# First feed forward's output product in Strassen's form, the norm after it fed by halves of the tokens, and two smaller rearrangements

## The chip, the cores and the metric

One NeuronCore of a Trainium2 chip runs the whole program. The metric is the device time of one execution in microseconds. In the profile PE is the matrix engine (TensorE), PEld its weight loads, DVE is VectorE, ACT is ScalarE, POOL is GpSimd, and SP is the engine whose queue starts nearly all transfers.

## The reference

One layer of a hybrid decoder, on 1024 prompt tokens and 32 sample tokens (8 sequences of 4), which the kernel treats as one block of T = 1056 columns. D is 1024, the feed forward's hidden width DFF is 2816, everything is float32.

```
x = x + 0.5 * SwiGLU_1(RMSNorm(x))
h = RMSNorm(x);  z = h @ w_in          # conv pair | q | k | v | gates
x = x + w_out( sigmoid(g_A) * conv(z) + sigmoid(g_B) * attention(z) )
x = x + 0.5 * SwiGLU_2(RMSNorm(x))
SwiGLU(h) = (silu(h @ w_gate) * (h @ w_up)) @ w_ffn_out
```

Outputs are x, the new keys and values, and the updated caches, most of them copies.

## The kernel before, in words

Features lie on the 128 partitions and tokens in the free dimension; x is eight tiles (KT = 8) of 128 x 1056. To keep float32 precision, each product of two float32 tiles is done as three TensorE products: both operands are split into a rounded high part (ACT, `activation` Copy into F32R) and a low remainder (a subtraction on DVE or POOL), and hi*hi, hi*lo and lo*hi are summed in PSUM. `weights` (L157), `split` (L183), `gemm` (L173) do this; the split of the weights is most of POOL's work.

The stages in order are these.

- **Start of the first feed forward**, `load_x` (L206). x comes in nine row blocks, is transposed on TensorE, and 1/rms of each token is a column that `scale(tb)` spreads over the partitions: ACT makes a diagonal matrix `dg` (L262), TensorE multiplies it by ones (L267), DVE copies the PSUM result to the SBUF row `rb` (L268). `apply` (L367) then makes h = x * gain * rb by one DVE instruction for each tile and block of 352 tokens (L373), its high part on ACT (L375) and its low part (L378). The hidden columns j = 0 and 1 are computed in the plain form, block by block (`lockstep` L444, `plain_gate`, `plain_up`, `plain_out` L468). `plain_last` (L476) does the last of these, splits its weights on DVE and issues `first_sums` (L542), the first weight sums of the next stage. The engines keep the program's order here (`in_order`, L117); what is issued after it, such as `combine` (L494), may be put between by the scheduler.
- **Hidden stage**, `hidden` (L430): for j = 2 to 21, `hidden_fast` (L553) does gate and up together by Strassen's form: 8 products of four K-tiles on two halves of 264 columns, 168 matmuls for each j. The sums of weights s1 to s4 (L564 to L567) and the four results `C` lie in one tile `q` of the tag "quad" (5 buffers), taken anew for each j.
- **Output product.** The first feed forward does it plainly, `ffn_out` (L804): 22 K-tiles in 4 chunks, 8 output tiles, 3 blocks of 352 columns, three products: 1584 matmuls. In the last chunk `after` calls `norm_feed` for each output tile and block: `scaled` (L354: a Copy on ACT, a remainder on DVE L359) and `square` (L382: ACT, and an addition on POOL L390 into the row `rbn`). The second feed forward does it by Strassen's form, `ffn_out_fast` (L661): K-tiles in pairs, in three passes of 4, 4 and 3 pairs, 7 products each, 4 output pairs o, two halves b of 264 columns, three products: 1848 matmuls. For that its hidden stage also forms differences of hidden rows on POOL (`hidden_pair` L624, L630 to L637) and stores them to `hx`. `acc` (L761) adds a product to x on DVE, `more` (L764) adds a kept term on POOL.
- **Mixer**: `norm_end` (L412) sums `rbn` over partitions, `qkv` (L1061), attention, convolution, gates, `branches`.
- **`mix_out`** (L1511): the mixer's output product, then 1/rms by `rms` (L392: a matmul with ones, a square root on ACT, a reciprocal on DVE L398, all on 128 x 352) and the start of the second feed forward in the same shape as `load_x`'s, in the order written out by hand.
- Hidden stage and `ffn_out_fast` of the second feed forward, the latter ending in `store_y` (transposes, L855).

Background work is issued by `later(n, ...)` n products ahead, `tick` counts products.

## Time and profile before

| | us |
|---|---|
| median of 3 runs | 2376.51 |
| lowest, highest | 2375.69, 2379.31 |
| the profiled execution | 2374.05 |
| its span | 2372.3 |

The span runs from the first to the last instruction of the profile; the execution's own time is 1.75 us more. A row of stretches gives, for each engine, its busy time and its instructions (x), then the granted TensorE clock as a share of full speed, the DMA engines' busy share and their rate. A row of waits says who waited for whom, the sum in us, how often, and the longest. A row of groups gives line, engine, operation, output<-inputs, shape, count, then busy us and mean ns of one, then idle us before them and what ended it. A row of the timeline gives start and length in us, and in brackets the idle time before it and what ended that.

### The profile page before, as it was taken

The page shows a single profiled execution, that of the slowest core. Times are in us where ns is not written, and L with a number is a line of the kernel's source. Part 1 is how long each engine was busy: PE and PEld are TensorE (multiplying, and loading weights), DVE is VectorE, ACT ScalarE, POOL GpSimd, SP SyncE. Part 2 cuts the span into 40 slices and gives each one's busy share as a digit, 9 for nine tenths or more (in the row PEclk, how much of TensorE's full clock was granted, in tenths as well). Part 3 has the DMA queues.
Part 4 walks back from the last instruction along what each step waited for, and adds up shares of the span by engine and source line. Part 5 has one row for each costly group of instructions (what it writes and reads, how often), then busy time and mean ns, then how long its engine had stood idle before and what let it go on. Part 6 is the DMA issues. An engine that isn't in the chain of part 4 may idle for free. (4 is left out here: it accounts for less than half of the span.)

```text
span 2372.3 us, 43139 instructions
## 1 busy us (share of the span) xinstructions
PE 2291.5 (97%) x16725; PEld 2231.9 (94%) x16725; DVE 1304.1 (55%) x2420; ACT 871.1 (37%) x2193; POOL 1143.6 (48%) x1070
## 2 busy tenths in 40 slices
PE   7999999999999999999999999998999999999998
PEld 7899999999999998987998999998999999999998
DVE  6755555542234635686666846418644434467765
ACT  5322222341125643643644234224332223234443
POOL 5644444453325512422421354545755555567676
PEclk8999999999999999999999999999999999999999
DMA  6222222273434212222243434631334333366323
GB/s 206 85 78 73 82 82 82 71 249 126 145 94 141 53 43 67 78 73 91 76 120 97 145 103 129 215 98 61 103 104 136 121 125 116 110 250 207 106 88 102
DMA packets 279705, 268.50 MB, mean 113 GB/s; under 512 B 21101, under 2 KB 254277, under 8 KB 277668
## 3 DMA queue, kind: packets, MB, share of 16 engines
q1 hardware_dynamic: 269292, 245.42, 32.5%
q10 hardware_dynamic: 10208, 20.32, 2.6%
q8 instruction: 132, 2.16, 0.4%
q14 instruction: 73, 0.60, 0.1%
HBM read 197.58 MB, written 87.27 MB: 120 GB/s over the span
## 5 line engine op out<-in xcount | busy, mean ns | idle before, releaser
L178 PE MATMUL mm<-h,wh 128*128 128x352 f32 x2256 | 566.2, 332 | 2.7 <-DVE t L1481 1.8
L578 PE MATMUL acc<-h,wh 128*128 128x264 f32 x2560 | 478.7, 287 | 23.5 <-DVE quad L587 14.8
L578 PEld LDWEIGHTS acc<-h,wh 128*128 128x128 f32 x2560 | 400.9, 190 | 28.1 <-issue 17.7
L178 PEld LDWEIGHTS mm<-h,wh 128*128 128x128 f32 x2256 | 401.6, 192 | 9.2 <-issue 2.6
L178 PE MATMUL mm<-h,wl 128*128 128x352 f32 x1128 | 371.9, 330 | 2.3 <-DVE wl L168 2.3
L578 PE MATMUL acc<-h,wl 128*128 128x264 f32 x1280 | 366.4, 286 | 0.0
L185 POOL TENSOR_TENSOR wl<-quad,wh 128x512 fp32r<-128x512 f32 x156 | 208.3, 1340 | 304.7 <-ACT wh L184 280.4
L578 PE MATMUL acc<-quad,wh 128*128 128x264 f32 x1920 | 354.5, 285 | 0.0
L168 POOL TENSOR_TENSOR wl<-wr,wh 128x512 fp32r<-128x512 f32 (+2 forms) x156 | 193.0, 1252 | 326.5 <-ACT wh L167 312.4
L578 PEld LDWEIGHTS acc<-quad,wh 128*128 128x128 f32 x1920 | 297.6, 188 | 0.2
L578 PE MATMUL acc<-quad,wl 128*128 128x264 f32 x960 | 272.7, 284 | 0.0
L578 PEld LDWEIGHTS acc<-h,wl 128*128 128x128 f32 x1280 | 243.2, 190 | 0.0
L754 PE MATMUL mm<-quad,wh 128*128 128x264 f32 x1232 | 230.3, 288 | 8.6 <-POOL quad L185 3.1
L1087 PE MATMUL mm<-wh,h 128*128 128x256 f32 x1152 | 219.8, 286 | 0.0
L178 PEld LDWEIGHTS mm<-h,wl 128*128 128x128 f32 x1128 | 217.0, 192 | 2.6 <-DVE wl L168 2.6
L184 ACT ACTIVATE wh<-quad 128x512 fp32r<-128x512 f32 x156 | 96.2, 628 | 304.9 <-DVE quad L565 165.6
L185 POOL TENSOR_TENSOR wl<-wr,wh 128x512 fp32r<-128x512 f32 x124 | 170.3, 1375 | 75.7 <-ACT wh L184 75.6
L754 PEld LDWEIGHTS mm<-quad,wh 128*128 128x128 f32 x1232 | 191.9, 189 | 11.1 <-issue 4.5
L1087 PEld LDWEIGHTS mm<-wh,h 128*128 128x128 f32 x1152 | 181.2, 189 | 1.2 <-issue 0.6
L578 PEld LDWEIGHTS acc<-quad,wl 128*128 128x128 f32 x960 | 180.6, 188 | 0.0
L754 PE MATMUL mm<-quad,wl 128*128 128x264 f32 x616 | 175.9, 286 | 1.4 <-POOL wl L185 1.4
L167 ACT ACTIVATE wh<-wr 128x512 fp32r<-128x512 f32 x196 | 107.7, 574 | 165.8 <-PE mm L178 101.1
(289 smaller groups left out, 4226.8 us busy)
## 6 DMA issues: line engine op xcount, KB each, us to landing
wr<-ffn_w_in SPq DMA_DIRECT2D x88, 512.0 KB
wr<-w_in SPq DMA_DIRECT2D x42, 512.0 KB
quad<-hx SPq DMA_DIRECT2D x74, 264.0 KB
xd<-quad SPq DMA_DIRECT2D x24, 528.0 KB
t<-hd SPq DMA_DIRECT2D x66, 176.0 KB
hd<-quad SPq DMA_DIRECT2D x20, 528.0 KB
hx<-quad SPq DMA_DIRECT2D x10, 1056.0 KB
quad<-xd SPq DMA_DIRECT2D x16, 528.0 KB
```

Source lines behind the costliest of these rows:

```text
L167: nc.scalar.activation(hi, raw[:, k:k + m, :], AF.Copy)
L168: ins = (eng or nc.gpsimd).tensor_tensor(out=lo, in0=raw[:, k:k + m, :], in1=f(hi), op=ALU.subtract)
L178: self.nc.tensor.matmul(ps[:, :BW], p, x[:, blk(tb)], start=(k == 0 and i == 0), stop=(k == nk - 1 and i == 2))
L184: self.nc.scalar.activation(hi, src, AF.Copy)
L185: return (eng or self.nc.vector).tensor_tensor(out=lo, in0=src, in1=f(hi), op=ALU.subtract)
L578: nc.tensor.matmul(acc[:, b, :HB], p[:, k, :], x[:, cols], start=(first and k == 0 and i == 0), stop=(k == 3 and i == 2), skip_group_check ...
L754: nc.tensor.matmul(ps[:, :HB], wp[:, k, :], q[:, s, k, cols], start=(k == 0 and i == 0), stop=(k == n - 1 and i == 2))
L1087: nc.tensor.matmul(ps[:m, :256], x, w, start=(k == 0 and j == 0), stop=(k == 7 and j == 2))
```

## The change

`build` calls `ffn_out_fast` for the first feed forward too, with its own last pass order, with `hx` rows in DRAM of its own, and with hooks that feed the mixer's norm by halves of the tokens. 1/rms is read by `apply` from PSUM. The tiles of `C` are taken twice and kept. `first_sums` is issued earlier, and every part of `combine` has to follow the split of u1.

```diff
+ORDER_END1 = ("P1", "P6", "P7", "P5", "P4", "P3", "P2")
@@ load_x
-        rb = self.rb = self.new_rb()
-            return lambda: nc.vector.tensor_copy(rb[:, 384 * tb:min(384 * tb + 384, T)], pb[:, :min(384, T - 384 * tb)])
+            return self.spread([(max(BW * tb - 128 * i, 0), min(BW * tb + BW - 128 * i, size(i)), rs[:, i:i + 1])
+                                for i in range(9) if 128 * i < BW * tb + BW and 128 * i + size(i) > BW * tb])
...
-            elif k == 7:
-                out.append(scale(2))
-        self.apply(gname, 1, second)
-        out.pop()()
+        self.apply(gname, 1, rb1, second)
         lock1 = self.lockstep(g0, u0, 1)
         for k in range(KT):
+            if k == 5:
+                rb2 = scale(2)
             lock1(k)
@@ apply
-                                               in1=self.rb[:, blk(tb)], op0=ALU.mult, op1=ALU.mult)
+                                               in1=rb[:, :BW], op0=ALU.mult, op1=ALU.mult)
+    def spread(self, parts):
+        pb = self.sc_ps()
+        n = 0
+        for a, b, col in parts:
+            dg = self.small(128, "dg", 3)
+            nc.scalar.activation(dg[:b, :b], self.ident[:b, :b], AF.Copy, scale=col[:b])
+            nc.tensor.matmul(pb[:, n:n + b - a], self.ones[:b, :], dg[:b, a:b], start=True, stop=True)
+            n += b - a
+        return pb
+    def square_half(self, k, h):
+        for t in (2 * HB * h, 2 * HB * h + HB):
+            x, s = self.xT[k][:, t:t + HB], self.rbn[:, t:t + HB]
+            if t not in self.squared:
+                self.squared.add(t)
+                nc.scalar.activation(s, x, AF.Square)
+            else:
+                sq = self.t352()[:, :HB]
+                nc.scalar.activation(sq, x, AF.Square)
+                nc.gpsimd.tensor_tensor(out=s, in0=s, in1=sq, op=ALU.add)
+    def scaled_half(self, gname, k, h):
+        sl = slice(2 * HB * h, 2 * HB * h + 2 * HB)
...
+        nc.scalar.activation(hi, x, AF.Copy, scale=g)
+        nc.vector.scalar_tensor_tensor(out=lo, in0=x, scalar=g, in1=f(hi), op0=ALU.mult, op1=ALU.subtract)
@@ plain_last
         self.u1_end = self.split_end
+        self.first_sums(w_in)
...
-            if tb == 1:
-                self.first_sums(w_in)
@@ combine
-            if k == 0:
-                self.after(ins, self.u1_end)
+            self.after(ins, self.u1_end)
@@ hidden_fast
-        q = self.quad().rearrange("p a t -> p (a t)")
+        if j < NREG + 2:
+            self.cs.append(self.quad().rearrange("p a t -> p (a t)"))
+        q = self.cs[j % 2]
...
+        if j == NREG:
+            self.after(ins, self.plain_end)
@@ ffn_out_fast
+            if last and p == end[0] and begin is not None:
+                begin()
+            ws = None
+            if middle is not None and step == len(order) - 1:
+                ws = [parts(o) for o in range(4)]
+                middle()
+            for o in range(4):
+                hi, lo = ws[o] if ws else parts(o)
...
                     if p == "P1":
-                        u[o, b] = self.t352()[:, :HB] if c else u12
-                        nc.scalar.activation(u[o, b], ps[:, :HB], AF.Copy, scale=0.25)
+                        u[o, b] = self.t352()[:, :HB] if c and not last else u12
+                        if last:
+                            acc(u12)
+                        else:
+                            nc.scalar.activation(u[o, b], ps[:, :HB], AF.Copy, scale=0.25)
...
                     elif p == "P6":
                         acc(u[o, b])
-                        if c:
+                        if c and not last:
                             more(u12, u[o, b])
                         if last:
                             more(x22, u12)
                     elif p == "P7":
+                        if last and end is not ORDER_END:
+                            more(x21, u12)
@@ qkv
-            for i in range(9):
+            for i in ((5, 6, 7, 8, 0, 1, 2, 3, 4) if g == 0 and kind == "q" else range(9)):
@@ mix_out
+        def rms(tb):
+            ps, r = self.tr_ps(), self.small(3, "r3", 2)
+            for i in range(3):
...
+                nc.tensor.matmul(ps[:m, i:i + 1], self.rbn[:, c:c + m], self.ones[:, 0:1], start=True, stop=True)
+                parts.append((0, m, r[:, i:i + 1]))
+            for m, c in ((128, slice(0, 2)), (BW - 256, slice(2, 3))):
+                nc.scalar.activation(r[:m, c], ps[:m, c], AF.Sqrt, scale=1.0 / D, bias=self.eps[:m])
+                nc.vector.reciprocal(r[:m, c], r[:m, c])
+            return lambda: self.spread(parts)
-        self.rms(0)()
-        left = [part(o, tb) for o, tb in ((6, 1), (7, 1), (5, 2))]
+        rb0 = rms(0)
+        left = [part(6, 1)]
+        rb0 = rb0()
+        left += [part(o, tb) for o, tb in ((7, 1), (5, 2))]
...
         p = self.plain_gate(w[2], 0)
+        rb.append(todo.pop(0)())
@@ build
+            self.hx = self.pairs("hy")
             self.hidden(a["ffn1_w_in"][0])
+            def final(o, h):
+                nc.sync.dma_start(out=self.xd[1][o][:, h * 2 * HB:h * 2 * HB + 2 * HB], in_=self.xT[o][:, h * 2 * HB:h * 2 * HB + 2 * HB])
+                self.square_half(o, h)
+                if o >= 4 or h == 0:
+                    self.scaled_half("mix_norm", o, h)
+            def middle():
+                for o in range(4):
+                    self.scaled_half("mix_norm", o, 1)
-            self.ffn_out(a["ffn1_w_out"][0], after, self.norm_begin)
+            self.ffn_out_fast(a["ffn1_w_out"][0], final, ORDER_END1, self.norm_begin, middle)
```

## Rows read from the trace of the kernel before

**Rows 1.** Stretches: starts, hidden stages, output products; PE, PEld, DVE, ACT, POOL.

```profile
0.00:88.98 88.98, 68.40 (x378) 65.58 (x379) 67.06 (x90) 45.47 (x91) 52.80 (x56) 0.88 0.48 154
88.98:505.50 416.52, 413.30 (x3360) 412.51 (x3360) 216.13 (x264) 127.25 (x217) 192.08 (x150) 0.99 0.29 91
505.50:761.90 256.40, 255.51 (x1585) 255.54 (x1585) 84.93 (x153) 73.58 (x162) 97.39 (x103) 1.00 0.44 142
...
1604.00:1683.98 79.98, 69.44 (x413) 67.89 (x411) 70.20 (x77) 35.91 (x68) 55.28 (x41) 0.97 0.17 56
1683.98:2114.50 430.52, 416.84 (x3360) 412.92 (x3360) 192.76 (x263) 130.94 (x228) 249.71 (x188) 0.99 0.38 127
2114.50:2206.17 91.67, 84.73 (x673) 83.63 (x673) 73.31 (x105) 37.32 (x67) 66.84 (x41) 0.98 0.68 230
2206.17:2290.04 83.87, 82.52 (x672) 81.95 (x673) 58.36 (x101) 34.29 (x62) 57.11 (x43) 1.00 0.29 94
2290.04:2372.30 82.26, 74.20 (x592) 71.11 (x592) 47.28 (x106) 30.45 (x62) 56.28 (x59) 1.00 0.35 103
```

**Rows 2.** Stretches without a stall inside the plain and the Strassen output product.

```profile
561.00:700.00 139.00, 139.00 (x865) 139.00 (x864) 37.04 (x70) 25.92 (x61) 42.42 (x46) 1.00 0.39 125
2242.68:2277.79 35.11, 35.11 (x288) 35.11 (x289) 21.46 (x42) 13.41 (x23) 27.41 (x23) 1.00 0.26 86
```

**Rows 3.** Groups on POOL by form, third pass of the Strassen output product.

```profile
L764 POOL TENSOR_TENSOR quad<-quad,wr 128x264 f32<-128x264 f32 x24 | 19.3, 814 | 0.5
L185 POOL TENSOR_TENSOR wl<-h,wh 128x384 fp32r<-128x384 f32 x17 | 17.7, 1047 | 5.0 <-ACT wh L184 5.0
L185 POOL TENSOR_TENSOR quad<-quad 128x528 fp32r<-128x528 f32 x10 | 13.6, 1368 | 0.0
```

**Rows 4.** Groups on DVE by form, last chunk of the plain output product.

```profile
L359 DVE SCALAR_TENSOR_TENSOR h<-quad,mix_norm,h 128x352 fp32r<-128x352 f32 x23 | 13.7, 598 | 14.0 <-ACT h L358 13.9
L838 DVE SCALAR_TENSOR_TENSOR quad<-mm,quad 128x352 f32<-128x352 f32 x25 | 13.1, 524 | 16.9 <-PE mm L178 16.9
```

**Rows 5.** Stretches: fourth and fifth product of the second feed forward's third pass.

```profile
2316.90:2330.21 13.31, 11.55 (x89) 10.46 (x88) 9.54 (x24) 5.40 (x10) 13.15 (x16) 1.00 0.30 89
2330.21:2344.14 13.93, 12.00 (x95) 10.87 (x93) 6.40 (x16) 5.20 (x11) 13.93 (x16) 1.00 0.42 123
```

**Rows 6.** Waits of PE and of DVE, second feed forward's hidden stage.

```profile
PE acc L578 <- DVE quad L587: 11.7, 10, 1.9
...
DVE quad L564 <- DMA hx<-quad: 36.8, 17, 4.1
```

**Rows 7.** Timeline of DVE and of PE, one such wait.

```profile
1890.56 0.69 DVE L564 TENSOR_TENSOR quad<-wr 128x512 f32<-128x512 f32 x1 [2.09 <-DMA hx<-quad]
...
1892.01 0.48 PE L578 MATMUL acc<-h,wh 128*128 128x264 f32 x2 [1.85 <-DVE quad L587]
```

**Rows 8.** Timeline of PE, first start: the longest idle time.

```profile
42.41 1.79 PE L267 MATMUL sc<-dg,ones 128*128 128x128 f32 x6 [6.41 <-ACT dg L262]
```

**Rows 9.** Stretches after the long idle times: first start, second start.

```profile
42.40:50.00 7.60, 7.58 (x32) 7.30 (x33) 6.03 (x10) 2.45 (x6) 2.58 (x3) 0.65 1.02 406
1655.00:1684.00 29.00, 24.64 (x142) 24.38 (x142) 26.13 (x30) 12.74 (x23) 22.52 (x14) 0.92 0.10 35
```

**Rows 10.** Waits of PE, end of the first start.

```profile
PE acc L578 <- DVE t L469: 2.4, 1, 2.4
```

**Rows 11.** Waits of PE, `mix_out` and second start.

```profile
PE mm L453 <- DVE t L460: 4.5, 1, 4.5
PE acc L578 <- DVE t L469: 4.2, 1, 4.2
```

**Rows 12.** Groups on DVE by form, second start, then first start.

```profile
L373 DVE SCALAR_TENSOR_TENSOR quad<-quad,ffn_norm,rb 128x352 f32<-128x352 f32 x24 | 21.8, 945 | 0.1
L398 DVE RECIPROCAL rb<-rb 128x352 f32<-128x352 f32 x3 | 7.0, 2348 | 2.6 <-ACT rb L397 2.5
...
L511 DVE TENSOR_TENSOR quad<-quad,quad 128x528 f32<-128x528 f32 x4 | 5.4, 1362 | 0.0
```

More of the change, by code (lines that the diff above doesn't have):

```diff
@@ L256, in scale @@
         def scale(tb):
-            d = []
-            for i in range(3 * tb, 3 * tb + 3):
-                m = size(i)
-                dg = self.small(128, "dg", 3)
-                nc.scalar.activation(dg[:m, :m], self.ident[:m, :m], AF.Copy, scale=rs[:m, i:i + 1])
-                d.append((i, m, dg))
-            pb = self.sc_ps()
-            for i, m, dg in d:
-                c = (i - 3 * tb) * 128
-                nc.tensor.matmul(pb[:, c:c + m], self.ones[:m, :], dg[:m, :m], start=True, stop=True)
-            return lambda: nc.vector.tensor_copy(rb[:, 384 * tb:min(384 * tb + 384, T)], pb[:, :min(384, T - 384 * tb)])
+            return self.spread([(max(BW * tb - 128 * i, 0), min(BW * tb + BW - 128 * i, size(i)), rs[:, i:i + 1])
+                                for i in range(9) if 128 * i < BW * tb + BW and 128 * i + size(i) > BW * tb])
         n0 = self.here()
@@ L275, in load_x @@
             turn(i)()
-        scale(0)()
+        rb0 = scale(0)
         g0, u0 = (self.weights(w_in[:, c:c + 128], KT, 128, sent=in_turn) for c in (0, DFF))
@@ L290, in first @@
                 out.append(turn(2 + k // 2))
-        self.apply(gname, 0, first, FIRST_K)
+        self.apply(gname, 0, rb0, first, FIRST_K)
         lock(KT - 1)
@@ L324, in third @@
                 keep.append(self.plain_swish(q))
-        self.apply(gname, 2, third)
+        self.apply(gname, 2, rb2, third)
         lock2 = self.lockstep(g0, u0, 2)
@@ L410, in norm_feed @@
         self.square(k, tb)
+    def square_half(self, k, h):
+        nc = self.nc
+        for t in (2 * HB * h, 2 * HB * h + HB):
[8 more added lines that the diff above has]
+    def scaled_half(self, gname, k, h):
+        nc = self.nc
+        if self.hn[k] is None:
+            self.hn[k] = (self.hrow(), self.hrow())
+        sl = slice(2 * HB * h, 2 * HB * h + 2 * HB)
+        x, g = self.xT[k][:, sl], self.gain[gname][:, k:k + 1]
+        hi, lo = (r[:, sl] for r in self.hn[k])
+        nc.scalar.activation(hi, x, AF.Copy, scale=g)
+        nc.vector.scalar_tensor_tensor(out=lo, in0=x, scalar=g, in1=f(hi), op0=ALU.mult, op1=ALU.subtract)
     def norm_end(self, cols):
@@ L438, in hidden @@
         self.two_banks()
+        self.cs = []
         for j in range(NREG, DFF // 128):
@@ L659, in pair_src, with ffn_out_fast @@
         return self.hx[i][t][:, r, :]
-    def ffn_out_fast(self, w_out, final):
+    def ffn_out_fast(self, w_out, final, end=ORDER_END, begin=None, middle=None):
         nc = self.nc
@@ L701, in ffn_out_fast @@
         X = {}
-        order = [(c, p) for c in range(len(PAIRS)) for p in (ORDER if c < len(PAIRS) - 1 else ORDER_END)]
+        order = [(c, p) for c in range(len(PAIRS)) for p in (ORDER if c < len(PAIRS) - 1 else end)]
         loads = []
@@ L742, in ffn_out_fast, with parts @@
                 load_x(*order[step + 2])
-            for o in range(4):
+            last = c == len(PAIRS) - 1
+            if last and p == end[0] and begin is not None:
+                begin()
+            def parts(o):
                 hi = self.P.tile([128, 4, 128], F32R, name=self.nm("wh"), tag="wh", bufs=6)
@@ L772, in ffn_out_fast @@
                         acc(x12)
-                        if last:
+                        if last and end is ORDER_END:
                             more(x21, u12)
@@ L1561, in first @@
             elif k == 7:
-                todo.pop(0)()
+                rb.append(todo.pop(0)())
                 w.append(weight(0))
                 left.append(part(7, 2))
-        self.apply(g, 0, first)
+        rb = []
+        self.apply(g, 0, rb0, first)
         left.pop(0)()
@@ L1577, in second @@
             elif k == 4:
-                todo.append(self.rms(2))
+                todo.append(rms(2))
             elif k == 5:
                 self.plain_up(lock0, 0, 0)
-            elif k == 8:
-                todo.pop(0)()
-        self.apply(g, 1, second)
+        self.apply(g, 1, rb[0], second)
         p = self.plain_gate(w[2], 0)
+        rb.append(todo.pop(0)())
         lock1 = self.lockstep(*w[:2], 1)
@@ L1593, in third @@
                 self.plain_up(lock1, 1, 0)
-        self.apply(g, 2, third)
+        self.apply(g, 2, rb[1], third)
         keep.append(self.plain_swish(self.plain_gate(w[2], 1)))
@@ L1641, in mixer, with pairs @@
         self.gates(0, 16, PR['gdrain'])
+    def pairs(self, name):
+        return [[self.DR.tile([128, n, 2 * HB], F32, name=f"{name}{i}_{n}") for n in (2, 4, 1)] for i in range(DFF // 256)]
     def build(self):
@@ L1675, in build @@
             self.mix_out(mg)
-            self.hx = [[self.DR.tile([128, n, 2 * HB], F32, name=f"hx{i}_{n}") for n in (2, 4, 1)] for i in range(DFF // 256)]
+            self.hx = self.pairs("hx")
             self.copy_caches(1, *COPY2)
```

18 lines of the change are left out of this document (9 added, 9 removed).

## The prediction

> **What bounds the kernel now.** I read the stretches first, cut at the borders of the stages, then the waits inside the stretches in which PE is not full, then the prices. PE is the bound almost everywhere: in the first hidden stage it is busy 413.30 of 416.52 us, in the plain output product 255.51 of 256.40. What it loses lies in few places: 20.6 us in the first start, 10.5 in the second, 13.7 in the second hidden stage, and 16.3 in the Strassen output product with its end [rows 1]. So a change pays either by fewer PE columns or by closing these holes, and this one does some of both.
>
> **The output product.** The plain form streams 1584 matmuls of 352 columns; an undisturbed stretch has 139.00 us for 864 of them, 160.9 ns each, so 254.8 us, about what the stage takes. The Strassen form needs 1848 of 264 columns; undisturbed, 288 take 35.11 us, 121.9 ns each [rows 2], so 225.3 us. PE alone would give back 30 us. The same code in the second feed forward shows how much of that survives. Its first pass takes 91.67 us where 672 x 121.9 ns are 81.9, its second 83.87 [rows 1]. I take both as they stand, since the first feed forward issues the same weight, x and operand transfers in the same order; the bounds are 10 us less in the first pass (its transfers arrive in time) and nothing more.
>
> The third pass is where the two feed forwards differ. PE needs 504 x 121.9 ns = 61.4 us. In the second feed forward it takes 82.26 us with 88 transposes and the end, and POOL is busy 56.28 us in it [rows 1]; its fourth and fifth products, 13.31 and 13.93 us instead of 8.8 and the transposes, have POOL busy all but 0.16 us [rows 5]. In the first, transposes fall away, but the norm comes in: 16 squares of half rows make 32 activations on ACT and 28 additions on POOL (the first of each quarter of the tokens needs none), and 16 `scaled_half` of 528 columns. An addition on 264 columns costs POOL 0.81 us by the nearest row, L764 [rows 3], so 22.8 us; the eight additions that P1's `acc` on DVE makes needless save 6.5. POOL then has 56.28 - 6.5 + 22.8 = 72.6 us of work against PE's 61.4. Its queue is in order and also makes the low parts of weights (1.05 us) and operands (1.37 us) [rows 3], which PE waits for. The last product's eight additions (6.5) can lie behind PE's end; 66 cannot. I take 70 us: 61.4 (nothing late) and 82 (see the rivals) are the bounds. Sum of the stage: 91.7 + 83.9 + 70 = 245.5 against 256.4, **-11 us**, between -31 and 0. That is a third of what PE alone promises.
>
> DVE has 47.28 us in the second feed forward's third pass [rows 1]; eight more `acc` and 16 remainders of 528 columns at 598 ns x 528/352 = 0.90 us [rows 4] add 3.2 and 14.4, so 65 us: nearly full too. Here a rule speaks against the change. The remainder of 352 columns with both tensors in SBUF takes 598 ns while POOL works half the time, one with an operand in PSUM 524 [rows 4], and `apply`'s with both in SBUF 945 where POOL is busier [rows 12]. The Trainium skill's page SBUF — State Buffer, section Who interferes with whom, says that a DVE instruction with two SBUF inputs and a GpSimd instruction that reads SBUF use one read interface, and that the later one waits for the whole of the other. By that rule DVE's 16 remainders would each wait out a POOL instruction; rival A prices this from the rows.
>
> The handover to the mixer: after the last product the chain is `acc`, square, addition for two halves, some 0.4 + 0.4 + 2 x 0.8 = 2.4 us, and the sums over partitions are issued behind one product of the mixer, 24 x 0.12 = 2.9 us. With POOL behind I book **+1.5**, between 0 and 6. The new order of q's tiles (5 to 8 first) only takes tokens that are ready; the x stores become 16 halves on SP's queue and the loads of q's weights lie among them: nothing, unless SP holds those loads behind the last stores, which is within the 6.
>
> **The first hidden stage** now forms the differences for Strassen: in the second feed forward these make POOL's time 249.71 instead of 192.08 us, and SP's traffic 127 instead of 91 GB/s [rows 1], both far from full. On PE they cost nothing by themselves: **+1**, between 0 and +14, the difference of the two hidden stages.
>
> **C's tiles kept.** The second hidden stage takes 430.52 us, the first 416.52, for the same 3360 matmuls [rows 1]. The 14 us are told by the waits: 17 times DVE's first weight sum (L564) stands 2.2 us on average until the store of hidden differences has left the tile that the new `q` gets, and PE then waits 10 times for a DVE addition (L587) queued behind it, 11.7 us [rows 6]. One case: DVE held until 1890.56, PE until 1892.01 [rows 7]. With two kept tiles the weight sums only have to wait for readers of their own columns, long done; the store matters for C's first writing, almost one j later. What is late next: the split of the weights on ACT, 1 to 2 us in all. **-13**, between -14 and 0. This is also why I book only +1 for the first.
>
> **The first start.** Four edits. PE stands 6.41 us for the diagonals of the third block [rows 8], because `scale(2)` is issued before `lock1`; now five K-tiles of it, 30 matmuls x 160.9 ns = 4.8 us, come ahead: -4.8. After that hole the granted clock is 0.65 of full for 7.6 us [rows 9], that is, most of it at the lower level of 1.2 GHz; 7.6 x 0.35 = 2.7 us, of which I take -2. The copy to `rb` goes and `apply` reads PSUM: 945 against 524 ns [rows 12, 4] in a DVE queue on which PE's first matmuls hang, -1. `first_sums` moved ahead and `combine` held back take up to 2.4 us [rows 10] and some of the wait for u1: -2. Against it: three of four rounds of `combine` that ran earlier, nine sums of up to 1.36 us [rows 12], now come behind u1, 12 us at most, while PE arrives 8 to 10 us earlier; the third product of the hidden stage wants them: +3. **-7**, between -12 and +3.
>
> **The second start** has the same frame. Its waits of 4.5 and 4.2 us [rows 11] both end on DVE; the three reciprocals of 2.35 us become ones on 128 x 2, and 24 instructions of 945 ns [rows 12] go to about 524 [rows 4], 17 us less on DVE in 80, of which it is busy 70.20 [rows 1]. ACT gets nine diagonals, PE nine small matmuls instead of six of 352: even. -7.5 for the waits (1.2 stays), -3 of the lower clock behind them (0.92 over 29 us [rows 9] are 2.3, and the 0.99 of the stage after it [rows 1] holds more), +3 for the late `combine`: **-7.5**, between -12 and +3.
>
> **The second output product's end.** The 6.5 us less on POOL fall where POOL is full and PE loses 5 us [rows 5]: **-3.5**, between -5 and 0.
>
> **Sum**: -11 + 1.5 + 1 - 13 - 7 - 7.5 - 3.5 = -39.5. From the profiled execution's 2374.05 (span 2372.3 and 1.75 around it) 2334.5; that execution lies 2.5 us under the median of the runs, so I say 2337.
>
> **Rivals.** A: DVE and POOL hold each other in the third pass. 16 remainders that each wait out a POOL instruction of 0.8 to 1.4 us [rows 3] put some 16 us on DVE's 65, and the pass becomes 81 to 82: 12 more, 2349. For it: both engines are nearly full there. Against: 598 ns in a chunk where POOL works half the time is little above the 524 with PSUM [rows 4]. 0.15. By the Trainium skill's rule this is the case; so far the traces bear it out only where POOL runs without a pause.
> B: the kept tile is followed as a whole. Then DVE stands for the store as now, the second hidden stage keeps its 14 us and the first gets them: 2337 + 13 + 13 = 2363. Against: the slots of x in the start are refilled while others of that tile are read. 0.07.
> C: the starts gain nothing, as `combine` behind u1 takes what the holes give: 2337 + 14.5 = 2351. For it: DVE is busy 70 of 80 us in the second [rows 1]. 0.14.
> D: nothing is late in the first product's passes: 2337 - 8 - 9 = 2320. 0.08.
> E, slower: POOL's queue serializes the third pass, a split for the next o standing behind an addition that waits for this o's product. A block then costs PE's 2.2 us and 0.4 + 0.4 + 0.8 + 1.05 = 2.65 us idle; 24 blocks from P6 on give 64, less the 8.6 already booked, 2392, more with the clock falling. It decides from about 18 blocks on. Against: splits run up to six tiles ahead, and the second feed forward's pass, with POOL as full for two products, loses 5 us [rows 5]. 0.03.
>
> **Numbers.** My forecast 0.53, A to E as given. The range takes in A, C and D's size, 2317 to 2360; B lies just above. Within 0.2% (about what a measurement can tell, 4.8 us) or slower needs E or several bounds at once: faster 0.94, same 0.03, slower 0.03.
>
> **What would show it.** Right: the first output product near 245 us with its loss in the third pass and POOL over 90% busy from P6 on; the waits of L564 for `hx` gone and both hidden stages near 417; no idle time over 2 us before `lock1` and before the second start's third block; the two starts some 80 and 71 us long. Wrong: L564 still waiting for stores, PE waiting in the hidden stages' first j for `combine`, or the mixer's first products waiting for POOL.

## The result, and the profile after

The changed kernel takes 2467.73 us (median of 4 runs), the kernel before 2377.81 beside it: a ratio of 1.0388, 95% interval 1.0359 to 1.0416. It is 90 us slower; 2337 was forecast. The profiled execution has a span of 2465.5 us against 2372.3. Its stretches, cut as in [rows 1]; the three passes of either output product stand apart:

```profile
0.00:91.37 91.37, 64.95 (x382) 62.03 (x383) 62.70 (x85) 46.28 (x93) 52.41 (x57) 0.89 0.44 143
91.37:506.96 415.59, 412.67 (x3360) 411.59 (x3360) 244.27 (x265) 135.22 (x228) 246.62 (x186) 0.99 0.33 109
507.96:639.27 131.31, 93.89 (x672) 90.58 (x672) 73.43 (x107) 35.55 (x64) 56.23 (x38) 0.87 0.58 197
639.27:766.64 127.37, 98.63 (x672) 95.58 (x673) 63.48 (x98) 33.22 (x61) 58.47 (x44) 0.84 0.29 95
766.64:855.36 88.72, 69.62 (x507) 67.35 (x506) 60.65 (x113) 42.19 (x88) 74.90 (x75) 0.88 0.34 112
...
1791.48:2207.16 415.68, 414.04 (x3360) 413.28 (x3360) 239.14 (x265) 129.05 (x227) 263.65 (x185) 1.00 0.41 131
2207.16:2465.50 258.34, 242.13 (x1936) 239.54 (x1936) 177.85 (x319) 100.06 (x184) 174.78 (x136) 0.97 0.45 145
```

The ledger by stage, the borders laid where TensorE's work changes:

| stage | before | after | difference | forecast |
|---|---|---|---|---|
| first start | 88.98 | 91.37 | +2.4 | -7 |
| first hidden stage | 416.52 | 415.59 | -0.9 | +1 |
| first output product with the handover | 256.40 | 352.64 (506.96 to 855.27, and 4.33 of waiting behind the mixer's first product) | +96.2 | -9.5 |
| mixer and second start | 922.08 | 931.88 (the rest up to 1791.48) | +9.8 | -7.5 |
| second hidden stage | 430.52 | 415.68 | -14.8 | -13 |
| second output product and end | 257.80 | 258.34 | +0.5 | -3.5 |

One line makes the result: the first output product. Its passes take 131, 127 and 89 us, where the same code in the second feed forward takes about 92, 84 and 82 (the last with transposes in place of the norm). TensorE is idle for 37, 29 and 19 us of them, and the granted clock is 0.84 to 0.88: between its holes TensorE runs part of the time at 1.2 instead of 2.4 GHz, so that 672 matmuls keep it busy for 93.89 us instead of some 84. Its waits in this stage (us in all, times, longest), and below them the largest of ScalarE:

```profile
PE mm L793 <- ACT wh L185: 51.5, 13, 11.6
PE mm L793 <- POOL wl L186: 14.7, 10, 4.8
...
PE tr L446 <- POOL rb L425: 4.3, 1, 4.3
...
ACT quad L185 <- DMA quad<-hy: 184.6, 32, 15.8
```

TensorE waits for the high halves of the weights, which ScalarE makes (L185); ScalarE waits 184.6 us in all for operand loads from `hy`. One such place, in the timelines of ScalarE, TensorE and SyncE's queue:

```profile
582.93 1.25 ACT L185 ACTIVATE quad<-quad 128x528 fp32r<-128x528 f32 x2 [14.76 <-DMA quad<-hy]
584.09 0.61 ACT L185 ACTIVATE wh<-h 128x512 fp32r<-128x512 f32 x1
584.97 1.26 ACT L185 ACTIVATE quad<-quad 128x528 fp32r<-128x528 f32 x2 [0.26 <-DMA quad<-hy]
585.60 0.52 ACTq L1511 DMA_DIRECT2D k_w_s<-cache_k_w  x1
586.14 0.61 ACT L185 ACTIVATE wh<-h 128x512 fp32r<-128x512 f32 x1
...
586.66 2.18 ACT L185 ACTIVATE wh<-h 128x512 fp32r<-128x512 f32 x4
...
584.76 0.81 PE L793 MATMUL mm<-quad,wh 128*128 128x264 f32 x2 [4.62 <-ACT wh L185]
...
580.16 1.75 SPq L744 DMA_DIRECT2D quad<-hy  x4
```

The four operand loads leave at 580.16, when TensorE has freed their tile, and TensorE runs dry at about the same moment (584.76 less 4.62). ScalarE has stood before the first of their splits for 14.76 us, and behind it in its queue, with copies of a cache between them, are the weight splits that TensorE wants now. In the second feed forward of the same execution ScalarE's timeline is mixed: a weight split every 2 to 3 us, with operand splits between them.

```profile
2325.43 0.63 ACT L185 ACTIVATE wh<-h 128x512 fp32r<-128x512 f32 x1 [2.28 <-PE mm L793]
2328.16 0.65 ACT L185 ACTIVATE quad<-quad 128x528 fp32r<-128x528 f32 x1 [2.09 <-DMA quad<-hx]
2328.71 0.62 ACT L185 ACTIVATE wh<-h 128x512 fp32r<-128x512 f32 x1
```

What differs is `copy_caches` (L1495): 18 copies from DRAM to DRAM, 9.86 MB, issued from ScalarE's queue and due one after every third product group from the first output product on. In the kernel before they lie in the same stage, and TensorE was idle for 0.9 us of it [rows 1].

Both hidden stages now start with one long wait, 16.3 us in the first and 16.4 in the second; before they were 2.4 and 4.2 [rows 10, 11]. VectorE has no pause there; the last plain output (L495), for which the first product of the hidden stage waits, stands behind the sums and splits of `combine`, here in the timelines of VectorE and TensorE:

```profile
80.38 1.80 DVE L535 TENSOR_TENSOR quad<-quad,quad 128x528 f32<-128x528 f32 x1
82.10 0.51 DVE L495 TENSOR_TENSOR t<-mm,t 128x352 f32<-128x352 f32 x1
...
83.83 6.96 DVE L529 TENSOR_TENSOR quad<-quad,quad 128x528 fp32r<-128x528 f32 x4
90.72 0.51 DVE L495 TENSOR_TENSOR t<-mm,t 128x352 f32<-128x352 f32 x1
...
91.37 0.78 PE L606 MATMUL acc<-h,wh 128*128 128x264 f32 x2 [16.27 <-DVE t L495]
```

### The profile page after: what moved, and what is told of

It is laid out like the page before. It is cut to its first block, busy times and chain, and to the rows that moved or that the text cites. A ratio compares the mean times of both kernels' runs of the same rounds, so it can differ in the third digit from the quotient of the medians.

```text
span 2465.5 us, 44269 instructions
## 1 busy us (share of the span) xinstructions
PE 2291.9 (93%) x17023; PEld 2228.4 (90%) x17023; DVE 1477.1 (60%) x2594; ACT 918.6 (37%) x2266; POOL 1305.6 (53%) x1158
## 5 line engine op out<-in xcount | busy, mean ns | idle before, releaser
L793 PE MATMUL mm<-quad,wh 128*128 128x264 f32 x2464 | 485.2, 297 | 73.6 <-ACT wh L185 51.5
L793 PEld LDWEIGHTS mm<-quad,wh 128*128 128x128 f32 x2464 | 406.8, 200 | 80.3 <-ACT wh L185 57.3
L179 PE MATMUL mm<-h,wh 128*128 128x352 f32 x1728 | 430.8, 330 | 1.9 <-DVE t L1524 1.8
L793 PE MATMUL mm<-quad,wl 128*128 128x264 f32 x1232 | 366.1, 297 | 21.6 <-POOL wl L186 14.7
L179 PEld LDWEIGHTS mm<-h,wh 128*128 128x128 f32 x1728 | 302.4, 190 | 7.4 <-issue 2.6
L793 PEld LDWEIGHTS mm<-quad,wl 128*128 128x128 f32 x1232 | 246.5, 200 | 25.5 <-POOL wl L186 17.3
L169 POOL TENSOR_TENSOR wl<-wr,wh 128x512 fp32r<-128x512 f32 x92 | 129.9, 1423 | 188.6 <-ACT wh L168 187.4
L186 POOL TENSOR_TENSOR wl<-wr,wh 128x512 fp32r<-128x512 f32 x124 | 181.5, 1465 | 77.4 <-ACT wh L185 77.4
L799 DVE SCALAR_TENSOR_TENSOR quad<-mm,quad 128x264 f32<-128x264 f32 x384 | 151.7, 424 | 105.4 <-PE mm L793 103.2
L186 POOL TENSOR_TENSOR quad<-quad 128x528 fp32r<-128x528 f32 x80 | 119.9, 1504 | 177.0 <-ACT quad L185 167.2
L186 POOL TENSOR_TENSOR wl<-h,wh 128x512 fp32r<-128x512 f32 (+1 forms) x126 | 176.7, 1416 | 43.1 <-ACT wh L185 26.8
L1130 PEld LDWEIGHTS mm<-wh,h 128*128 128x128 f32 x1152 | 184.6, 192 | 3.4 <-ACT mm L1190 1.1
```

Source lines behind the costliest of these rows:

```text
L169: ins = (eng or nc.gpsimd).tensor_tensor(out=lo, in0=raw[:, k:k + m, :], in1=f(hi), op=ALU.subtract)
L179: self.nc.tensor.matmul(ps[:, :BW], p, x[:, blk(tb)], start=(k == 0 and i == 0), stop=(k == nk - 1 and i == 2))
L186: return (eng or self.nc.vector).tensor_tensor(out=lo, in0=src, in1=f(hi), op=ALU.subtract)
L793: nc.tensor.matmul(ps[:, :HB], wp[:, k, :], q[:, s, k, cols], start=(k == 0 and i == 0), stop=(k == n - 1 and i == 2))
L799: nc.vector.scalar_tensor_tensor(out=y, in0=ps[:, :HB], scalar=0.25 * sign, in1=y, op0=ALU.mult, op1=ALU.add)
L1130: nc.tensor.matmul(ps[:m, :256], x, w, start=(k == 0 and j == 0), stop=(k == 7 and j == 2))
```

## The experiments

All runs beside runs of the kernel before. The medians of these lie between 2371 and 2377 us, so two rows of the table compare by their ratios better than by their times:

| run | us | ratio to before, 95% interval |
|---|---|---|
| copies_hidden | 2381.45 | 1.0040, 1.0024 to 1.0056 |
| copies_ordered | 2402.81 | 1.0123, 1.0098 to 1.0148 |
| none_bunched | 2380.25 | 1.0020, 1.0009 to 1.0030 |
| none_bunched2 | 2479.06 | 1.0449, 1.0427 to 1.0470 |
| plain_out | 2369.66 | 0.9971, 0.9959 to 0.9984 |
| plain_starts | 2362.50 | 0.9954, 0.9936 to 0.9971 |
| plain_oldstart | 2351.28 | 0.9907, 0.9892 to 0.9922 |
| best1 | 2365.06 | 0.9965, 0.9946 to 0.9984 |
| fast_clean | 2362.25 | 0.9932, 0.9913 to 0.9950 |
| fast_stores | 2357.85 | 0.9907, 0.9890 to 0.9925 |
| fast_sums | 2355.45 | 0.9905, 0.9889 to 0.9922 |
| fast_order | 2355.63 | 0.9929, 0.9905 to 0.9953 |
| clean_loads | 2359.49 | 0.9946, 0.9931 to 0.9960 |
| fast_loads | 2351.41 | 0.9923, 0.9900 to 0.9947 |
| fast_pool | 2349.10 | 0.9900, 0.9869 to 0.9931 |
| fast_mix | 2388.40 | 1.0054, 1.0035 to 1.0073 |

### The copies: their order or their traffic

```diff
+            self.copy_caches(0, *COPY1)      # COPY1 = (17, 5)
             self.hidden(a["ffn1_w_in"][0])
...
-            self.copy_caches(0, *COPY1)      # COPY1 = (10, 3)
             self.ffn_out_fast(...)
```

> The edit: the first feed forward's part of the cache copies (issued on ScalarE's queue, one after every third product group of the output product) is due in the hidden stage instead, one after every fifth group. Theory ORDER: the copies between the steps of the output product changed the order that the planner lays down on ScalarE: four operand splits, which wait for their load, then the weight splits that TensorE needs first. Without copies there the order is mixed again as in the second feed forward; the output product falls from about 354 us to 245 to 260 and the total to 2360 to 2380. Rival TRAFFIC: the 9.9 MB of copies delay the operand loads themselves; the same gain here. Rival FORM: the output product in this form is slow here for another reason (the norm's squares and sums on POOL, the third pass): the total stays at 2440 or more.

2381.45, 1.5 us above the range of ORDER: 86 us come back. Below, the stretch of the first hidden stage and those of the three passes: the first two are now what was forecast (91.7 and 83.9), the third is not (70); the hidden stage is 10 us longer.

```profile
90.78:515.95 425.17, 417.20 (x3360) 415.09 (x3360) 240.23 (x265) 132.85 (x228) 256.07 (x186) 0.99 0.40 130
...
516.84:607.34 90.50, 84.38 (x673) 83.44 (x673) 71.42 (x104) 37.08 (x67) 65.26 (x40) 0.98 0.68 228
607.34:691.00 83.66, 82.32 (x673) 81.75 (x673) 59.26 (x101) 34.43 (x62) 57.03 (x43) 1.00 0.30 94
691.00:770.37 79.37, 65.38 (x505) 63.78 (x506) 58.26 (x113) 40.89 (x85) 71.33 (x72) 0.91 0.36 120
```

ORDER and TRAFFIC both fit this, so the next run leaves the copies where they were and changes the order alone:

```diff
-                self.split(f(lo), hi, lo, ...)          # in load_x, for the step after next
+                lag.append((order.index((c, p)), hi, lo, ...))
...
                 hi, lo = ws[o] if ws else parts(o)
+                if lag and lag[0][0] <= step + 1:
+                    split_x()      # ACT's part behind the last weight split
```

> The edit: the copies stay where the changed kernel has them, all bytes too, but in the first output product each operand split is traced one step later and ordered behind a weight split, so that ScalarE's queue has weight and operand splits in turn (copies between them). ORDER: 2365 to 2390, nearly all of what moving the copies gives. TRAFFIC: 2440 to 2470, since the loads land as late as before.

It lies between the two, nearer to ORDER: 65 of the 86 us come back with every byte in place. The passes, in order of time:

```profile
507.48:613.61 106.13, 87.14 (x673) 85.69 (x673) 66.37 (x102) 35.39 (x65) 58.95 (x40) 0.92 0.69 236
613.61:702.81 89.20, 84.55 (x674) 83.45 (x673) 55.91 (x102) 32.83 (x62) 54.07 (x43) 0.98 0.46 148
702.81:786.81 84.00, 67.12 (x507) 65.54 (x506) 58.61 (x114) 40.90 (x86) 73.73 (x73) 0.90 0.36 118
```

16 us of the rest are in the first pass, where weights, x and copies are all loaded. Most of that is one wait of 12.9 us for an operand split on VectorE; the profile names a cache copy as what the load of these operands had waited for, 11.3 us on SyncE's queue:

```profile
PE mm L808 <- DVE quad L747: 13.5, 2, 12.9
...
SPq L754 <- DMA k_w_s<-cache_k_w: 11.3, 1, 11.3
```

The Trainium skill's page Trainium Kernel Development and Optimization, section Key Constraints, says that transfers issued from the different engines' queues run on the same 16 DMA engines and interleave; the busier first pass (DMA share 0.69 over 106 us against 0.68 over 90) agrees with it.

The reverse is the order without the copies.

> The edit: the first feed forward's part of the cache copies is left out altogether (that half of the copied caches is not written), and by hand each step's second to fourth weight splits on ScalarE are ordered behind the operand splits of the next step, so that ScalarE's queue shows four operand splits and then four weight splits without any copy. ORDER: the gaps of 4 to 5 us per step are back, 2430 to 2480. TRAFFIC: 2350 to 2375, since nothing delays the loads.

```diff
+                if end is not ORDER_END and step > 1 and o > 0 and step + 1 in xdone:
+                    self.after(ins, xdone[step + 1])   # none_bunched2: xdone[step + 2]
```

ORDER had put 2430 to 2480 on this run; at 2380.25 the loss did not appear. But that run did not have the changed kernel's order: it held a step's weight splits behind operands whose loads had begun a step earlier. In the changed kernel they are the operands of the step after next.

> The edit: the first feed forward's part of the cache copies is left out again (that half of the copied caches is not written). In the run none_bunched the operand splits that stood ahead of a step's weight splits belonged to the next step, whose load had begun a step earlier; in the changed kernel they belong to the step after next, whose load begins only when the step itself begins. Here each step's second to fourth weight splits stand behind the operand splits of the step after next. ORDER: the gaps of 4 to 5 us per step are back and the output product takes 320 to 350 us, total 2440 to 2470. TRAFFIC: 255 to 262 us as in none_bunched, total 2375 to 2385.

2479.06, without one byte of these copies: the stretches of the three passes, then the longest waits of TensorE and ScalarE.

```profile
507.19:636.55 129.36, 97.32 (x673) 94.77 (x674) 74.34 (x104) 34.23 (x62) 56.95 (x38) 0.84 0.48 161
636.55:770.13 133.58, 103.79 (x675) 100.25 (x674) 69.46 (x99) 33.98 (x62) 56.83 (x43) 0.81 0.18 59
770.13:870.57 100.44, 76.01 (x508) 73.63 (x507) 65.17 (x113) 43.51 (x90) 76.95 (x78) 0.83 0.28 95
```
```profile
PE mm L800 <- ACT wh L783: 71.8, 17, 10.3
...
ACT quad L747 <- DMA quad<-hy: 179.7, 31, 15.0
```

The second pass moves 59 GB/s instead of 95 and takes 6 us longer than in the changed kernel. So the order by itself makes a loss of this size, gaps, low clock and all. With the order mended some 20 us stay lost beside the copies (2402.81 against 2381.45); whether their traffic or their place in the queues does that was not taken apart. The framework lays down each queue ahead of the run; what in the copies made it choose that order was not tried.

### The starts

```diff
-            self.ffn_out_fast(a["ffn1_w_out"][0], final, ORDER_END1, self.norm_begin, middle)
+            self.ffn_out(a["ffn1_w_out"][0], after, self.norm_begin)      # and hx = None
```

> The edit: the first feed forward's output product is in the plain form again, with the norm fed by blocks of 352 tokens as before; all other parts of the change stay. If the whole loss is in that product, the total falls by its 354 less 256, to 2365 to 2372: 13 us below before from the kept tiles in the second hidden stage and little from the two starts. If the starts lose by themselves (both wait 16 us for VectorE ahead of the hidden stage), it stands at 2378 or more; if they gain as forecast (14 us), at 2350.

2369.66, 0.3% under before: the kept tiles pay (second hidden stage 413.17 us), the starts do not; each still waits 16.3 us for L495. From here, two ways of ordering the start:

> The edit: from plain_out, VectorE's part of the operand splits that the hidden stage needs third and later, and the combination of the fourth pair of rows, are ordered behind the last plain output (plain_end), so that VectorE reaches that output sooner. Theory BACKLOG (both hidden stages start 16 us late because the last plain output stands in VectorE's queue behind the whole of the combinations): each gap falls from 16.3 to 3 to 8 us, total 2345 to 2357. Rival NEEDED (the hidden stage's second and third products need those combinations at once, so the wait only moves behind the first product): 2365 to 2372, with new gaps of 5 to 10 us behind the first two products of each hidden stage.

> The edit: from plain_out, the three edits to the order ahead of the hidden stage are undone: the first sums behind the second of the last plain products again, only the first combination ordered behind the last weight split, the fourth sum free. 1/rms from PSUM and the kept tiles stay. BACKLOG as a fault of the new order: combinations run while TensorE is still at the plain products, the gap at each start falls to 3 to 9 us, total 2350 to 2362. If VectorE's amount of work alone sets the start, whatever its order: gaps of 14 to 17 us stay, 2366 to 2373.

```diff
-        self.first_sums(w_in)                 # plain_oldstart: back behind the product of tb == 1
-            self.after(ins, self.u1_end)      # for every k; plain_oldstart: for k == 0 alone
-            self.after(ins, self.plain_end)   # on s4
```

plain_starts, 2362.50, lies between the two ranges: the wait falls to 4.7 us, but the first hidden stage grows from 416.76 to 424.84, its first 31 us at a clock of 0.85 with TensorE busy for 26.67; BACKLOG and NEEDED are both right in part. plain_oldstart is better than both others: 2351.28, at the low end of its range. First the stretches of plain_starts, the beginning of its first hidden stage and the whole; then those of plain_oldstart, first start, first and second hidden stage. The waits for L495 are down to 3.6 and 4.5 us in plain_oldstart:

```profile
79.22:110.00 30.78, 26.67 (x177) 25.46 (x178) 22.45 (x23) 10.22 (x18) 22.53 (x17) 0.85 0.31 92
79.22:504.06 424.84, 417.57 (x3360) 415.74 (x3360) 239.40 (x273) 130.53 (x222) 199.61 (x155) 0.98 0.28 91
```
```profile
0.00:85.19 85.19, 67.22 (x383) 63.78 (x383) 61.50 (x87) 45.52 (x93) 50.34 (x56) 0.94 0.50 161
85.19:500.18 414.99, 411.83 (x3360) 411.11 (x3360) 228.56 (x263) 127.09 (x217) 190.62 (x150) 1.00 0.28 90
...
1676.78:2090.50 413.72, 411.14 (x3360) 409.85 (x3360) 243.23 (x263) 129.79 (x228) 267.15 (x188) 1.00 0.41 132
```

So the three edits to the order cost some 16 us (plain_out is 6.3 us under the runs of before beside it, plain_oldstart 22.5); with them undone, 1/rms from PSUM and the kept tiles make the kernel 1% faster than before.

### What the Strassen form is worth without the copies

> The edit: from copies_hidden, the first feed forward's copies come after every seventh product group (not every fifth), the start order of plain_starts, and in the first output product's norm feed the second of each two additions of squares goes to VectorE instead of POOL. Expected: the first hidden stage 416 us instead of 425 (gaps of 1 to 2 us beside copies gone), the stall of 11.5 us in the third pass down to 0 to 6, each start 8 to 13 us shorter if BACKLOG holds: 2335 to 2355. If NEEDED holds, 2360 to 2370; if the stall in the third pass isn't POOL's backlog, 11 us stay there.

2365.06, above the range for BACKLOG and inside that for NEEDED: the start order of plain_starts lost again behind the start, and the first hidden stage takes 426 us, not 416. In the third pass TensorE's waits now name VectorE's additions to x (L801), 10.6 us in all and 6.8 at the longest; near that wait VectorE itself stands for 8.31 us before one of the additions of squares moved to it. The rest builds on the start order of plain_oldstart.

> The edit: the changed kernel with its cache copies in the first hidden stage (after every seventh product group) and the three edits to the start order undone as in plain_oldstart; the first output product in Strassen's form, 1/rms from PSUM and the kept tiles stay. Against plain_oldstart (2351) it tells what the Strassen form is worth once the planner's order is right. If the form brings what was forecast (11 us less in the passes, 1.5 lost at the handover): 2338 to 2343. Rival THIRD PASS (POOL's additions and squares and the stores of x stand ahead of what TensorE needs, 11.5 us of stall in copies_hidden, and the handover waits for the last squares): it is worth nothing, 2348 to 2356.

2362.25 is above both ranges. As THIRD PASS said, there is no gain: the ratio to before is 0.9932, that of plain_oldstart 0.9907. The third pass takes 78.89 us. SyncE's, ScalarE's and TensorE's longest waits in it:

```profile
SPq L162 <- POOL quad L802: 18.3, 2, 12.0
...
ACT t L424 <- POOL quad L802: 13.5, 1, 13.5
...
PE mm L793 <- ACT h L434: 11.8, 2, 11.5
```

The first two end on POOL's additions (L802), and TensorE's wait is for ScalarE, which stood behind them. Three ways from POOL to TensorE were taken away one after the other, each on top of the one before:

> The edit: from fast_clean, the stores of x ahead of the mixer leave SyncE's queue in the third pass and follow behind the last operand load. If these stores (each waits for its tile's last addition) held back the operand loads behind them, the stall in the third pass falls from about 11 us to below 5 and the total is 5 to 10 us under fast_clean. If POOL's backlog itself holds ScalarE's squares and the weight splits behind them, the stall stays and the total is within 3 us of fast_clean.

> The edit: from fast_stores, in the third pass of both output products POOL's addition of the common sum to x22 and x21 is merged into the step of P7: VectorE forms the common sum plus P7 once and adds it to x21, POOL adds it to x22; eight additions of 0.8 us fewer on POOL in each product, as many on VectorE as before. If POOL's backlog is what stalls the third pass, the stall is gone and the total is 5 to 12 us under fast_clean, the second output product 1 to 3 us shorter too. If not, within 2 us of fast_stores.

> The edit: from fast_sums, in the last four steps of the first output product ScalarE's squares and scaled halves of a finished tile are put off by a step and ordered behind the weight splits of the running step and the first two of the next. Theory IN LINE (ScalarE's squares wait for POOL's last additions and the weight splits stand behind them on ScalarE; fast_stores showed that the stores of x do not hold anything): the stall of 7.2 us falls below 2 and the total is 4 to 8 us under fast_sums, 2347 to 2352, unless the squares put off come out at the handover, which then grows from 4.3 to 8 or more and takes it back. Rival: POOL's splits of the weights (the low halves) are themselves late, whatever ScalarE does: the stall stays at 5 to 8 us.

```diff
-                nc.sync.dma_start(out=self.xd[1][o]..., in_=self.xT[o]...)     # fast_stores: behind the last operand load
-                            more(x22, u12)                                     # fast_sums: P7 adds v = P7/4 + u12
-                        final(oo, h)                                           # fast_order: a step later, ACT's part
+                            pending.append((oo, h))                            #   behind the weight splits
```

The stall stays at 11.5 us in fast_stores (the stores hold nothing), falls to 7.2 in fast_sums (eight additions fewer), and is 9.3 in fast_order, where ScalarE now waits for the last operand loads; these stand on SyncE behind the mixer's first weight loads, which wait for the tiles of the common sums. The totals are 2357.85, 2355.45 and 2355.63: fast_order misses its range, and the second output product, which fast_sums was to shorten too, takes 253.9 us from its first matmul to the end of the span in fast_stores and in fast_sums.

> The edit: from fast_clean, the mixer's weight loads are ordered behind the last operand load of the first output product on SyncE's queue; nothing else. Theory LOADS (the mixer's first two weight loads take tiles that hold the common sums, so they wait on SyncE's queue for POOL's last additions, 18.3 us in fast_clean, and the last step's operand loads stand behind them): the stall of 11.5 us shrinks to 0 to 6, total 2350 to 2358. Rival SQUARES (ScalarE's square waits 13.5 us for POOL's addition, with the weight splits behind it): the stall stays at 9 to 12 us, total 2358 to 2365.

> The edit: from fast_order (squares behind the weight splits, merged sums, stores behind the loads), the mixer's weight loads are ordered behind the last operand load. With both holds taken away the stall of 9.3 us should fall below 2 and the total to 2341 to 2349, under plain_oldstart (2351); if the squares and sums that were put off then hold the handover, it grows from 3 to 8 or more and the total stays at 2350 to 2356.

clean_loads gives 2359.49, inside the range of SQUARES, fast_loads 2351.41, above its range. In clean_loads the stall changes its name and keeps its size; TensorE's waits now name POOL alone:

```profile
PE mm L797 <- POOL wl L189: 10.8, 3, 5.3
```

The loads and the squares were ways by which POOL's backlog reached TensorE, not its cause. In fast_loads, with all of them closed, 7.9 us of waiting for POOL's low halves and 3.9 at the handover are left.

> The edit: from fast_loads, the second of each two additions of squares in the norm feed goes to VectorE instead of POOL (14 of 28 additions, 12 of which were POOL's at 0.7 to 1.0 us). Theory POOL (with the loads and ScalarE's order out of the way, the stall of 7.9 us and the handover of 3.9 us are POOL's own amount of work at the end): both shrink, together from 11.8 to 2 to 6 us, total 2343 to 2348. Rival: VectorE takes it back (its evictions stand behind the additions, PSUM fills): the stall is then named after VectorE and the total stays at 2349 to 2354.

With half of the additions of squares on VectorE the total is 2349.10, just above the range of POOL and at the low end of the rival's. The stretches of the first hidden stage and of the third pass, first in fast_loads, then in fast_pool, and below them TensorE's waits in fast_pool:

```profile
84.10:502.11 418.01, 411.17 (x3360) 409.81 (x3360) 240.87 (x263) 129.54 (x228) 266.60 (x188) 1.00 0.41 131
675.90:749.32 73.42, 64.34 (x506) 63.16 (x504) 58.01 (x111) 41.16 (x84) 65.30 (x61) 0.93 0.34 115
```
```profile
84.18:507.70 423.52, 416.77 (x3360) 415.40 (x3360) 240.51 (x263) 130.27 (x229) 267.11 (x189) 0.98 0.41 132
680.82:753.39 72.57, 65.21 (x505) 63.24 (x505) 67.52 (x122) 41.00 (x86) 61.43 (x55) 0.98 0.33 113
```
```profile
PE mm L813 <- DVE quad L819: 5.2, 5, 1.9
PE mm L813 <- POOL wl L789: 2.1, 1, 2.1
...
PE tr L449 <- POOL rb L428: 0.6, 1, 0.6
```

Both sides are right in part. The waits for POOL fall from 8.4 us in the pass and 3.9 at the handover to 2.1 and 0.6. In the pass, waits for VectorE (L819) take their place, and it is only 0.85 us shorter (73.42 to 72.57), with VectorE busy for 67.52 us of it. So the work on POOL was what held the third pass up, and once a part of it is moved, the work on VectorE holds it up too.

From the end of the hidden stage to the next one fast_pool takes 1162.9 us (507.70 to 1670.65), plain_oldstart 1176.6 (500.18 to 1676.78): 13.7 us for the Strassen form. All of it is in the product, 245.5 us up to the mixer's first matmul (at 753.23) against 259.3 (759.44). But fast_pool's first hidden stage is 8.5 us longer than plain_oldstart's, and 2349.10 against 2351.28 (0.9900 against 0.9907) is no difference that these runs can tell. Of the 8.5 us, 5.5 do not come from that stage's code: fast_loads has the same code up to there and takes 418.01 us, with TensorE busy for 411.17 us at a clock of 1.00 instead of 416.77 at 0.98.

> The edit: from fast_pool, the first feed forward's cache copies are due in the first part of the mixer, one after every second product group, instead of the first hidden stage. If the hidden stage paid for the copies and the mixer hides them: hidden stage back from 423 to 415, total 2339 to 2345. Rival: the mixer's planner order and its own loads pay instead (its weights are loaded just in time on SyncE's queue): the hidden stage gets shorter, the mixer longer by as much, total 2347 to 2356.

2388.40: neither. The hidden stage without copies takes 421.31 us, between those of fast_loads and fast_pool with them, so these runs do not show that the copies cost it anything (why all three are longer than plain_oldstart's 414.99 stays open); and the mixer, with the copies in it, loses time, as its stretch from 850 to 1100 shows:

```profile
850.00:1100.00 250.00, 224.33 (x1546) 204.94 (x1546) 155.12 (x427) 92.36 (x366) 74.72 (x96) 0.93 0.24 75
```

In fast_pool TensorE is busy 243.43 of these 250 us, at a clock of 0.99 and nearly the same traffic (69 GB/s). Whether order or traffic does it there was not taken apart.

## Why the prediction was wrong, step by step

**The first two passes** (forecast 91.7 and 83.9, measured 131.3 and 127.4: 83 of the 131 us by which the forecast was missed). The step that failed: "I take both as they stand, since the first feed forward issues the same weight, x and operand transfers in the same order". The transfers of the product are the same; the list was not complete. 18 cache copies are due in this stage, in plain sight in the kernel, and beside them the queue of ScalarE came out in another order. With the copies in the hidden stage the two passes take 90.5 and 83.7, so the prices were right and the order they rest on was not. No rival named this; E, the slower one, had TensorE serialized by POOL.

**The third pass** (70, measured 88.7; 79.4 with the copies in the hidden stage). POOL's backlog was forecast; its size was not, nor its way to TensorE. The mis-sized term is POOL's 72.6 us of work: in copies_hidden POOL is busy for 79.36 us from the start of this pass to the end of the last addition of squares (691.00 to 778.40). Such an addition was priced at 0.81 us after L764 [rows 3]; it took 1.0 on average and 1.2 in the median, in the changed kernel's row of that line (ns: minimum, median, maximum):

```profile
L425 POOL TENSOR_TENSOR rb<-rb,t x28: 731/1196/1313, 820.3 to 862.6; 128x264 f32<-128x264 f32 x28
```

28 of them are 27.7 us in all in the changed kernel, not 22.8. And the longest wait, 11.5 us in copies_hidden, is not for the low halves of which the prediction speaks: TensorE waits there for ScalarE, whose square waits 13.5 us for POOL, with the weight splits behind it. How the 9 us divide between price and way is not shown; the edits up to fast_loads take 5.5 us off the pass (78.89 to 73.42), the 14 additions taken off POOL in fast_pool 0.85 more. The product as a whole then takes 245.5 us, as forecast, but after several more edits, and with the first two passes some 3 us under their forecast and the third as much over it, which is luck. The price of VectorE's remainders held: 0.98 us for L435 against 0.90.

**The handover** (+1.5, up to 6): 4.3 us of waiting, on POOL as said.

**The first hidden stage** (+1): -0.9. **C's tiles kept** (-13): -14.8 in the changed kernel, -16.8 in plain_oldstart (430.52 to 413.72); VectorE's waits for `hx` [rows 6] are gone and TensorE waits 1.6 us in all for L615 in the changed kernel. Right.

**The starts** (-7 and -7.5): the holes closed as forecast, the 6.41 us of [rows 8] among them, and the waits that rival C names took all of it and more: 16.3 and 16.4 us. The failed step is "+3 for the late `combine`", argued from when the third product needs it; what it delays is the last plain output in VectorE's own queue, and that releases the first product. The 2 us booked as a gain for "`first_sums` moved ahead and `combine` held back" were a loss: without these edits and the one to s4 the kernel is some 16 us faster, the first start gains 3.8 us (88.98 to 85.19), and the second with the mixer 4.7 (922.08 to 917.34, in plain_oldstart).

**The second output product's end** (-3.5): +0.5. POOL has 174.78 us to do instead of 180.23 [rows 1], but the stage is no shorter. The step that failed is that 6.5 us less on POOL give PE 3.5 back: in the third pass POOL is busy for 49.55 us instead of 56.28, and the pass takes 81.31 us instead of 82.26.

**A's rule.** VectorE's sums of 528 columns (L535) in the first start took 0.69 to 1.80 us; POOL's additions of squares took 0.73 us in copies_hidden while VectorE stood still, and up to 1.33 where it ran. The Trainium skill's page SBUF — State Buffer, section Who interferes with whom, has a VectorE instruction with two SBUF inputs and a GpSimd instruction that reads SBUF take one interface in turn; both rows agree. So rival A was right in kind, but its price came on POOL's additions and not on VectorE's remainders, which took 0.98 us where A gave each the length of a POOL instruction on top.

## What to carry to other kernels

When a stage is forecast from another stage with the same code, list everything else that is due in it, on every queue: ScalarE's queue ran in order here, and one split that waited 14.76 us for its load decided for all behind it. A product that should have become 11 us shorter became over 90 us longer, because weight splits came to stand behind a load that TensorE's own progress releases. Before moving work "behind" an instruction, look which later instruction on that same engine releases the next stage.

## What was not expected of the hardware

With waits of 4.2 us on average (none_bunched2: 17 of them, 71.8 us) the granted clock was 0.81 to 0.84 over whole passes: in the second, 672 matmuls were busy for 103.79 us against 82.32 for as many at 1.00 in copies_hidden. That is 21 us on top of 30 us of idle time, so each us of hole went with 0.7 us more of slower matmuls. And the same 264-column addition on POOL ranged from 731 to 1313 ns within one stage.
